# Stores of the second half's products, outputs and sums issued some steps later, pools that wait tile by tile, and four places for the front's sums

## The chip, the cores and the metric

The kernel runs on one core of one Trainium2 chip. The metric is the device time of one execution in microseconds (us); lower is better. All data starts and ends in HBM. The engines are TensorE (PE, with its weight loads as PEld), VectorE (DVE), ScalarE (ACT), GpSimd (POOL) and SyncE (SP). SP does no arithmetic here: it issues every DMA of the kernel, one after the other, from one queue.

## The reference, cut to what matters

One sequence of 1024 tokens with 1024 channels passes two layers, in fp32:

```python
for l in range(2):
    h = rms_norm(x, g0) * (1 + sc_m) + sh_m
    if l == 0: y = conformer_conv(h)             # 1024 -> 2048, GLU, causal conv of 31, layer norm, silu, 1024 -> 1024
    else:      y = diff_attention(h, k, v)       # k, v = rms_norm(x) @ w_k, @ w_v
    x = x + g_m * rms_norm(y, g1)
    h = rms_norm(x, g2) * (1 + sc_f) + sh_f
    y = conv_ffn(h)                              # u = conv3(h @ w_in): 1024 -> 2*2816;  (silu(g) * v) @ w_out
    x = x + g_f * rms_norm(y, g3)

def diff_attention(h, k, v):                     # 8 heads, two score maps each, causal
    q = h @ w_q
    s = q_c . k_c * scale + bias(distance)       # c = 0, 1
    a = softmax(s_0) - lam * softmax(s_1)
    return rms_norm(a @ v) * (1 - lambda_init) @ w_o
```

## The kernel before

**Products.** A matmul operand in fp32 is split into a rounded part and a remainder (`whi`, `wlo` of a weight, `hT` and its pair of an activation; in the second half `wh`, `wl`), and each product is three matmuls: high by high, high by low, low by high. ACT rounds (L207, L1044), POOL or DVE subtracts (L208, L1045).

**Halves.** The 1024 tokens are worked on in two halves of 512. Layer 0, the projections to Q, K and V and the first half of layer 1 are the *front part*: they are recorded in loops and put in order by the framework's scheduler, in pools opened on the stack `front` (`fc`, `wp`, `big`, `at`, `pre` and three of PSUM). `front.close()` ends them, and the *back part* begins with new pools over the same bytes: `back`, `ab`, and `psc`, `ptr`, `pav`, `pf` in PSUM. The back part holds the second half's attention, its output projection and the last FFN.

**The last FFN by sums.** The last FFN's up and down projections are formed from seven products of sums of blocks instead of eight plain ones. The sums of the weights' blocks are made on POOL and kept in HBM. `front_sums` makes those of `w_out` (11 steps of `sums_t`: two tiles of 128 x 1024 loaded, four subtractions at L940, two stores `ftd` at L942 and L943) and those of 12 of the 22 blocks of `w_in` (`sums_s`: two tiles loaded, subtractions at L951 to L957, three stores `sxd`, `syd`, `s1d` at L958 to L960), spread over the first half's attention and FFN. The other 10 are made by `First.sums` while the second half's attention runs, with the tiles `rx`, `ry` and `S`.

**The second half's attention** is written out in its order by hand (`manual_schedule`): the framework keeps each engine's instructions as the loop issues them. The loop runs over 32 steps, four for each head (one of 128 queries each), with 5 more to empty it. Step i takes the maxima of query block i (DVE), turns block i-2 (PE transposes L1203, ACT copies, DVE), exponentiates block i (ACT), issues the scores of block i+1 (PE, L1162) and, in even steps, the values of two blocks (PE, L1222 to L1224). In odd steps `First.unit` adds 12 matmuls of the last FFN (L1105 to L1107) into a bank of PSUM; every second unit, once a head, ACT copies the finished bank to a tile `X` (L1108) and it is stored as `fdx` (L1110).

In HBM, Q, K, V and the bias lie as `qd`, `kd`, `vd` and `gd`, the transposed normed rows for the last FFN as `hfd`.

**The order on SP's queue** in that loop is the order of the calls. `load_kq(h+1)` issues four loads each of Q and K (L1141, L1142) and one of the bias strip `BW` at the start of the second step of head h; `load_v(h)` issues four loads of V (L1151) at the start of its first; then come, where they fall, the store of the attention output `od` (L1227, in even steps, after ACT's copy L1226), the store `fdx`, the loads of `rx` (L1072) and `ry` (L947) and the stores of the three sums. SP is in order: a store at its head that waits for ACT or POOL holds every load behind it. Each DMA also carries one of eight numbered lanes (DMAHW0 to DMAHW7) in turn and waits until the DMA eight issues ahead of it has landed. Tiles of 4 KB a partition (Q, K, `rx`, `ry`, `X`) share 13 places, the tag `q`.

Of the kernel before, what the change touches and what calls it, by code (L numbers as in the profile page):

```python
# [12 lines left out]
F32 = mybir.dt.float32  # L13
# [6 lines left out]
P = 128  # L20
S = 1024
# [7 lines left out]
FC = F // P  # L29
# [43 lines left out]
NWS, NSS, NQ, NHS = 12, 6, 13, 40  # L73
LA = 5
LAT = 4
QS = 10


# [34 lines left out]
def trunk(ctx: ExitStack, tc: tile.TileContext, x, mw, cols, grow, w1, w2, wk, wv, wq, wo, win, wout, relb, onehot, lamr, out):  # L113
    nc = tc.nc
    V, A, G, T = nc.vector, nc.scalar, nc.gpsimd, nc.tensor
    dma = nc.sync.dma_start
    PSUM = bass.MemoryType.PSUM
# [14 lines left out]
    def nm(s):  # L132
        uid[0] += 1
        return f"{s}_{uid[0]}"
# [250 lines left out]
    def gate_row(l, v, g, r, gdr=None):  # L385

        m = sm(8)
        yield from mod_col(l, v, m)
        V.tensor_tensor(out=m, in0=m, in1=col("normg", (l * 4 + g) * 8, 8), op=ALU.mult)
        if gdr is None:  # L390
            gdr = dr.tile([1, D], F32, name=nm("gdr"))
        dma(out=gdr[0].rearrange("(k p) -> p k", p=P), in_=m)
        if r is not None:
            dma(out=r, in_=gdr.broadcast_to([P, D]))
# [215 lines left out]
    for c in range(KC):  # L610
        g = conv(cv, c, nxt.pop(0), cA, sumA, TA, py, "y")
# [64 lines left out]
    od = [[dr.tile([P, 512], F32, name=f"od{h}_{half}") for half in range(2)] for h in range(NH)]  # L676
# [248 lines left out]
    ftd = [[dr.tile([P, D], F32, name=f"ftd{j}_{i}") for i in range(2)] for j in range(FC // 2)]  # L925
    sxd, syd = [[dr.tile([P, D], F32, name=f"{n}{q}") for q in range(FC)] for n in ("sxd", "syd")]
    s1d = [dr.tile([P, 512], F32, name=f"s1d{q}") for q in range(FC)]
# [2 lines left out]

        return t.rearrange("p (k two j) -> p two k j", two=2, j=P)

    def sums_t(j, u, v):

        dma(out=u, in_=wout[1, 0, j])
        dma(out=v, in_=wout[1, 1, j])
        yield
        u0, u1, v0, v1 = u[:, 0:512], u[:, 512:1024], v[:, 0:512], v[:, 512:1024]
        for o, a, b in ((u0, v0, u0), (v0, v1, v0), (v1, v1, u0), (u1, u1, v1)):
            G.tensor_tensor(out=o, in0=a, in1=b, op=ALU.subtract)  # L940
            yield
        dma(out=ftd[j][0], in_=u)  # L942
        dma(out=ftd[j][1], in_=v)  # L943

    def sums_s(q, x, y, s):

        dma(out=y, in_=win[1, q + FC])  # L947
        yield
        (x0, x1), (y0, y1) = [[blocks(t)[:, i] for i in range(2)] for t in (x, y)]
        s_ = s.rearrange("p (k j) -> p k j", j=P)  # L950
        G.tensor_tensor(out=s_, in0=y0, in1=y1, op=ALU.add)  # L951
        yield
        G.tensor_tensor(out=y0, in0=x0, in1=y0, op=ALU.subtract)
        yield
        G.tensor_tensor(out=x0, in0=s_, in1=x0, op=ALU.subtract)
        yield
        G.tensor_tensor(out=x1, in0=x1, in1=x0, op=ALU.subtract)  # L957
        dma(out=sxd[q], in_=x)  # L958
        dma(out=syd[q], in_=y)
        dma(out=s1d[q], in_=s)  # L960
        yield

    def front_sums():
        def p4():
            return pre_.tile([P, 1024], F32, tag="p4", bufs=2, name=nm("p4"))
        for j in range(FC // 2):
            yield from sums_t(j, p4(), p4())
        for q in range(QS, FC):
            x = p4()
            dma(out=x, in_=win[1, q])  # L970
            yield from sums_s(q, x, p4(), pre_.tile([P, 512], F32, tag="p2", bufs=1, name=nm("p2")))

    pre_ = front.enter_context(tc.tile_pool(name="pre", bufs=1))
    gd_m1, gd_f1 = [dr.tile([1, D], F32, name=f"gdrow{n}") for n in range(2)]
# [4 lines left out]
    f = ffn(0, 1, hB, yB, gn_f0, ssB)  # L979
    interleave(itertools.islice(f, 60), (attn(at, 0, ssqA), NAT, 0, AE),  # L980
               (chain(gate_row(1, 2, 1, gn_m1, gd_m1), mod_scale(1, 4, 2, s_f1), mod_col(1, 3, sh_f1),
                       gate_row(1, 5, 3, None, gd_f1)), 32, 0, 60), (front_sums(), 5 * (FC // 2) + 6 * (FC - QS), 0, 60))
    ynA = wo_norm(ssqA)
    actA = []
    alongside(f, wo_pre(0, ynA, gpair, actA))
# [6 lines left out]
    front.close()  # L992


    back = ctx.enter_context(tc.tile_pool(name="back", bufs=1))
    att = ExitStack()
    ab = att.enter_context(tc.tile_pool(name="ab", bufs=1))
    psc = att.enter_context(tc.tile_pool(name="psc", bufs=2, space=PSUM))
    ptr = att.enter_context(tc.tile_pool(name="ptr", bufs=1, space=PSUM))
    pav = att.enter_context(tc.tile_pool(name="pav", bufs=1, space=PSUM))  # L1000
    pf = att.enter_context(tc.tile_pool(name="pf", bufs=1, space=PSUM))
    opool, bpool = [None], [None]

    def b2k(name="s"):
        return back.tile([P, 512], F32, tag="s", bufs=NSS, name=nm(name))

    def b4k(name="q", dt=F32):
        return back.tile([P, 1024], dt, tag="q", bufs=NQ, name=nm(name))
# [54 lines left out]
    fdx = [dr.tile([P, D], F32, name=f"fdx{q}") for q in range(FC)]  # L1063

    class First:
# [20 lines left out]
        def sums(self, q):  # L1086

            x = self.raws.pop(q)
            if q < QS:
                yield from sums_s(q, x, b4k("ry"), b2k("S"))  # L1090

        def unit(self, mk):

            q, i = divmod(self.u, 2)
            self.u += 1
            if q >= FC:
                return
            if i == 0:
                self.ps, self.x = mk(), b4k("X")
            hi, lo = self.pairs.pop((q, i))  # L1100
            ps = self.ps
            for j in range(4):
                ah, al = H[1 + i][j]
                w, v = hi[:, j * P:(j + 1) * P], lo[:, j * P:(j + 1) * P]
                T.matmul(ps, lhsT=w, rhs=ah, start=(i == 0 and j == 0), stop=False, skip_group_check=True)  # L1105
                T.matmul(ps, lhsT=w, rhs=al, start=False, stop=False, skip_group_check=True)
                T.matmul(ps, lhsT=v, rhs=ah, start=False, stop=(j == 3), skip_group_check=True)  # L1107
            A.copy(self.x[:, (1 - i) * 512:(2 - i) * 512], ps)  # L1108
            if i == 1:
                dma(out=fdx[q], in_=self.x)  # L1110

    first = First()
    bg = []

    def tick(n=1):
        for _ in range(n):
# [30 lines left out]
    def load_v(h):  # L1147
        Vh = [ab.tile([P, 8, P], F32R, tag=f"V{hl}", bufs=2, name=nm("V")) for hl in range(2)]
        for hl in range(2):
            for half in range(2):  # L1150
                dma(out=Vh[hl].bitcast(F32)[:, half * NT:(half + 1) * NT, :],  # L1151
                    in_=vd[half][:, :, hl, h * P:(h + 1) * P].rearrange("k p e -> p k e"))
        VV[h] = Vh
# [61 lines left out]
    def values(h, pr):  # L1215

        ah, al = AV[pr]
        nkb = NT + 2 * pr + 2
        po = pav.tile([P, 512], F32, tag="av", name=nm("Pav"))
        Vh = VV[h]  # L1220
        for kb in range(nkb):
            T.matmul(po[:, 0:256], lhsT=Vh[0][:, kb, :], rhs=ah[:, kb, :], start=(kb == 0), stop=False, skip_group_check=True)  # L1222
            T.matmul(po[:, 0:256], lhsT=Vh[0][:, kb, :], rhs=al[:, kb, :], start=False, stop=False, skip_group_check=True)
            T.matmul(po[:, 0:256], lhsT=Vh[1][:, kb, :], rhs=ah[:, kb, :], start=False, stop=(kb == nkb - 1), skip_group_check=True)  # L1224
        o = b2k("o")
        A.copy(o[:, 0:256], po[:, 0:256])  # L1226
        dma(out=od[h][1][:, pr * 256:(pr + 1) * 256], in_=o[:, 0:256])  # L1227
        sq = b2k("sq")
        A.activation(sq[:, 0:256], po[:, 0:256], AF.Square)
        return po, sq  # L1230
# [35 lines left out]
    for i in range(NTL + 5):  # L1266
        if i % NT == 1 and i // NT + 1 < NH:
            load_kq(i // NT + 1)
        if i % NT == 0 and i < NTL:
            load_v(i // NT)  # L1270
        if i < NTL:
            maxima(i)
        if 0 <= i - 2 < NTL:
            turned(i - 2)
        if i < NTL:
            exps(i)
        if i + 1 < NTL:
            scores(i + 1, 0)
            scores(i + 1, 1)
        t = i - 3  # L1280
        if i % 2 == 0 and 0 <= t < NTL:
            pairs[t] = values(t // NT, (t % NT) // 2)
        if t - 1 in pairs:
            squares(*pairs[t - 1])
        more(i)
        if 0 <= i - 2 < NTL:
            turned_lo(i - 2)
        if 0 <= i - 1 < NTL:
            difference(i - 1)
        if t - 1 in pairs:  # L1290
            V.tensor_copy(ss[:, t - 2:t], pairs.pop(t - 1)[0][:, 256:258])


    v = bsm(NTL)
    V.scalar_tensor_tensor(out=v, in0=r0, scalar=2.0 * HD * EPS, in1=r0, op0=ALU.mult, op1=ALU.mult)
# [1 line left out]
    yn = bnewton(v, NTL)  # L1297
    inorder.__exit__(None, None, None)
    att.close()
    opool[0] = ctx.enter_context(tc.tile_pool(name="op", bufs=1))  # L1300
    bpool[0] = ctx.enter_context(tc.tile_pool(name="bp", bufs=1, space=PSUM))


    bplan["pool"] = 0.4
# [51 lines left out]
    y, ss2 = [b4k("y") for _ in range(NT)], bsm(8)  # L1356
# [25 lines left out]
    for nh in range(2):  # L1382
        ps = [bank("Py") for _ in range(NT)]
        for pr in range(4 if nh == 0 else 2):
            w = wo_weights(nh, pr)
# [9 lines left out]
    w = [wo_weights(1, pr) for pr in (2, 3)]  # L1395
# [146 lines left out]
    y, ss2 = [], bsm(16)  # L1542
# [29 lines left out]
    n, late = FC // 2, 6  # L1572
# [127 lines left out]
```

## Time and profile before

| | |
|---|---|
| median of 3 runs | 2668.21 us (2660.86 to 2669.43) |
| the profiled execution | 2669.41 us |
| its span in the trace | 2667.6 us |
| PE busy, share of the span | 2400.3 us, 90% |
| DVE, ACT, POOL busy | 72%, 43%, 36% |
| DMA traffic | 499.54 MB, mean 187 GB/s |
| mean granted clock of TensorE | 0.963 |

The span runs from the first to the last instruction of one execution, on which all rows below are taken; the time of the execution is 1.8 us longer. "Busy" counts instructions in work; the granted clock is the share of full speed (1.00 is 2.4 GHz, 0.50 is 1.2 GHz), averaged over a stretch. Idle time in a row is put down to what ended it: `<- DMA K<-kd` is a wait that ended when a load of K landed.

### The profile page before, as it was taken

What the parts mean: (1) busy time and instruction counts of PE and PEld (TensorE: products, weight loads), DVE (VectorE), ACT (ScalarE), POOL (GpSimd) and SP (SyncE); (2) the same over time, 40 slices, a digit from 0 to 9 for tenths busy, and PEclk for the clock granted to TensorE, in tenths of its full rate; (3) what the DMA queues carried; (4) which work ended last, traced back from release to release, by engine and by line L of the source; (5) the groups of instructions that cost most, each with busy time, mean ns of one, the idle gap of its engine ahead of it and who ended that gap; (6) DMA issues with size and microseconds to landing.
All of it is one profiled execution on the core that took longest, in us unless ns stands there. A gap on an engine that the chain in (4) does not pass through costs nothing. (4 is left out here: it accounts for less than half of the span.)

```text
span 2667.6 us, 30514 instructions
## 1 busy us (share of the span) xinstructions
PE 2400.3 (90%) x10346; PEld 1887.5 (71%) x10346; DVE 1924.2 (72%) x3072; ACT 1137.7 (43%) x1871; POOL 962.3 (36%) x578
## 2 busy tenths in 40 slices
PE   5998889999988988898889999787899899999997
PEld 4666667777766766776767777576777677777875
DVE  6998689999778346757757771366664799997556
ACT  4434244332444235535534352254543544444543
POOL 2234334444534453554544323142242211213221
PEclk9999999999999998999999999898999999999999
DMA  7123643434345776677776356688863645555656
GB/s 274 56 64 111 216 163 103 156 121 128 103 140 186 268 270 201 223 252 231 237 234 231 126 184 195 193 242 239 222 230 119 234 174 186 190 197 193 198 184 218
DMA packets 204811, 499.54 MB, mean 187 GB/s; under 512 B 24432, under 2 KB 64752, under 8 KB 204656
## 3 DMA queue, kind: packets, MB, share of 16 engines
q1 hardware_dynamic: 204656, 497.60, 57.2%
q8 instruction: 82, 1.34, 0.2%
q14 instruction: 73, 0.60, 0.1%
HBM read 375.61 MB, written 121.91 MB: 187 GB/s over the span
## 5 line engine op out<-in xcount | busy, mean ns | idle before, releaser
L208 POOL TENSOR_TENSOR wlo<-raw,whi 128x1024 fp32r<-128x1024 f32 x204 | 509.3, 2498 | 758.3 <-ACT whi L207 738.1
L207 ACT CAST whi<-raw 128x1024 fp32r<-128x1024 f32 x234 | 244.9, 1047 | 466.9 <-issue 249.2
L228 PE MATMUL Pu<-hT,whi 128*128 128x512 f32 x832 | 341.6, 411 | 27.1 <-DVE tap L426 16.7
L230 PE MATMUL Pu<-hT,wlo 128*128 128x512 f32 x832 | 338.7, 407 | 12.7 <-POOL wlo L208 10.9
L229 PE MATMUL Pu<-hT,whi 128*128 128x512 f32 x832 | 337.7, 406 | 3.3 <-DVE hT L308 3.2
L493 DVE SCALAR_TENSOR_TENSOR Pcv<-cu,sv,Pcv 128x512 f32<-128x512 f32 x432 | 299.8, 747 | 3.5 <-PE Pcv L488 2.6
L243 PE MATMUL Py<-whi,gT 128*128 128x512 f32 x608 | 247.6, 408 | 15.6 <-DVE yf L447 9.5
L244 PE MATMUL Py<-wlo,gT 128*128 128x512 f32 x608 | 244.2, 402 | 7.7 <-POOL wlo L208 7.7
L245 PE MATMUL Py<-whi,gT 128*128 128x512 f32 x608 | 243.1, 400 | 0.5 <-DVE gT L185 0.5
L228 PEld LDWEIGHTS Pu<-hT,whi 128*128 128x128 f32 x832 | 161.3, 194 | 71.0 <-issue 20.4
L230 PEld LDWEIGHTS Pu<-hT,wlo 128*128 128x128 f32 x832 | 161.3, 194 | 55.2 <-POOL wlo L208 14.6
L363 DVE CUSTOM_DVE_ANT_0 mraw<-mraw,crow 128x1024 f32<-128x1024 f32 x96 | 149.1, 1554 | 68.0 <-DMA mraw<-in_mw_dram 67.9
L229 PEld LDWEIGHTS Pu<-hT,whi 128*128 128x128 f32 x832 | 161.4, 194 | 41.3 <-DVE hT L308 4.5
L243 PEld LDWEIGHTS Py<-whi,gT 128*128 128x128 f32 x608 | 116.8, 192 | 45.3 <-issue 14.5
L244 PEld LDWEIGHTS Py<-wlo,gT 128*128 128x128 f32 x608 | 116.9, 192 | 36.0 <-POOL wlo L208 9.9
L245 PEld LDWEIGHTS Py<-whi,gT 128*128 128x128 f32 x608 | 116.4, 191 | 28.3 <-DVE gT L185 1.0
L1045 DVE TENSOR_TENSOR op<-raw,op 128x512 fp32r<-128x512 f32 x115 | 91.8, 823 | 60.9 <-ACT op L1044 53.6
L1044 ACT CAST op<-raw 128x512 fp32r<-128x512 f32 x154 | 93.1, 621 | 85.4 <-DMA raw<-fad 27.9
L1589 PE MATMUL Py<-op,op 128*128 128x512 f32 x308 | 121.6, 395 | 6.7 <-ACT op L1044 5.8
L1590 PE MATMUL Py<-op,op 128*128 128x512 f32 x308 | 122.2, 397 | 4.3 <-POOL op L1045 3.5
L1591 PE MATMUL Py<-op,op 128*128 128x512 f32 x308 | 121.0, 393 | 0.0
L1045 POOL TENSOR_TENSOR wl<-rx,wh 128x512 fp32r<-128x512 f32 x44 | 58.1, 1338 | 169.8 <-ACT wh L1044 169.5
(327 smaller groups left out, 5715.3 us busy)
## 6 DMA issues: line engine op xcount, KB each, us to landing
mraw<-in_mw_dram SPq DMA_DIRECT2D x96, 512.0 KB, 5.0
raw<-in_win_dram SPq DMA_DIRECT2D x88, 512.0 KB, 4.1
raw<-in_w_dram SPq DMA_DIRECT2D x48, 512.0 KB, 3.6
raw<-in_wout_dram SPq DMA_DIRECT2D x44, 512.0 KB, 4.0
raw<-fad SPq DMA_DIRECT2D x77, 256.0 KB, 3.8
K<-kd SPq DMA_DIRECT2D x48, 256.0 KB, 7.2
V<-vd SPq DMA_DIRECT2D x48, 256.0 KB, 6.0
p<-in_win_dram SPq DMA_DIRECT2D x24, 512.0 KB, 5.4
```

The source lines that it names most:

```text
L207: A.copy(hi, raw)
L208: e.tensor_tensor(out=lo, in0=raw, in1=hi.bitcast(F32), op=ALU.subtract)
L228: T.matmul(ps, lhsT=a, rhs=ah, start=(k == 0), stop=False)
L229: T.matmul(ps, lhsT=a, rhs=al, start=False, stop=False)
L230: T.matmul(ps, lhsT=b, rhs=ah, start=False, stop=(k == KC - 1))
L243: T.matmul(ps[t], lhsT=a, rhs=rh, start=(f == 0), stop=False)
L244: T.matmul(ps[t], lhsT=a, rhs=rl, start=False, stop=False)
L245: T.matmul(ps[t], lhsT=b, rhs=rh, start=False, stop=(f == n - 1))
L363: V.tensor_tensor_reduce(out=raw, in0=raw, in1=crow, scale=1.0, scalar=0.0, op0=ALU.mult, op1=ALU.add, accum_out=r[:, k:k + 1])
L493: V.scalar_tensor_tensor(out=ps, in0=u[:, j:j + 512], scalar=col("dw", j * 8 + c), in1=ps, op0=ALU.mult, op1=ALU.add)
L1045: e.tensor_tensor(out=lo, in0=src, in1=hi.bitcast(F32), op=ALU.subtract)
L1590: T.matmul(ps[t], lhsT=a, rhs=bl, start=False, stop=False, **more_)
```

## The change

Three parts. First, the pools of the back part, and `op` and `bp` that follow it, are opened with `reuse_waits="tile"`: a tile waits for the tiles whose bytes it takes over, not for all that lay in the closed pools. Second, in the second half's attention the stores are put on a list and issued at the head of a later step, behind that step's loads: `fdx` and `od` one step later, the three sums two steps later. Third, `front_sums` has four places for its 4 KB tiles instead of two and two for its 2 KB tile instead of one, and holds the stores of one step until the next step has issued its loads.

```diff
+NPRE = 4
...
-    def sums_t(j, u, v):
+    def sums_t(j, u, v, st):
...
-        dma(out=ftd[j][0], in_=u)
-        dma(out=ftd[j][1], in_=v)
+        st(ftd[j][0], u)
+        st(ftd[j][1], v)
...
-        dma(out=sxd[q], in_=x)
-        dma(out=syd[q], in_=y)
-        dma(out=s1d[q], in_=s)
+        st(sxd[q], x)
+        st(syd[q], y)
+        st(s1d[q], s)
...
-    def front_sums():
+    def front_sums(js, qs):
+
         def p4():
-            return pre_.tile([P, 1024], F32, tag="p4", bufs=2, name=nm("p4"))
-        for j in range(FC // 2):
-            yield from sums_t(j, p4(), p4())
-        for q in range(QS, FC):
+            return pre_.tile([P, 1024], F32, tag="p4", bufs=NPRE, name=nm("p4"))
+        held = []
+
+        def st(out, in_):
+            held.append((out, in_))
+
+        def flush(n):
+            while len(held) > n:
+                o, i = held.pop(0)
+                dma(out=o, in_=i)
+        for j in js:
+            g = sums_t(j, p4(), p4(), st)
+            next(g)
+            flush(0)
+            yield
+            yield from g
+        for q in qs:
...
-    back = ctx.enter_context(tc.tile_pool(name="back", bufs=1))
+    back = ctx.enter_context(tc.tile_pool(name="back", bufs=1, reuse_waits="tile"))
...
-                yield from sums_s(q, x, b4k("ry"), b2k("S"))
+                yield from sums_s(q, x, b4k("ry"), b2k("S"), lambda o, i: store(o, i, 2))
...
-                dma(out=fdx[q], in_=self.x)
+                store(fdx[q], self.x)
...
+    def store(out, in_, steps=1):
+
+        if now[0] is None:
+            dma(out=out, in_=in_)
+        else:
+            waiting.append((now[0] + steps, out, in_))
+
+    def stores(step):
+
+        now[0] = step
+        due = [w for w in waiting if step is None or w[0] <= step]
+        waiting[:] = [w for w in waiting if step is not None and w[0] > step]
+        for _, o, i in due:
+            dma(out=o, in_=i)
...
-        dma(out=od[h][1][:, pr * 256:(pr + 1) * 256], in_=o[:, 0:256])
+        store(od[h][1][:, pr * 256:(pr + 1) * 256], o[:, 0:256])
...
         if i % NT == 0 and i < NTL:
             load_v(i // NT)
+        stores(i)
         if i < NTL:
             maxima(i)
```

**One head on SP's queue.** The next two pieces are SyncE's rows from one head's last `od` store to the middle of the next head's Q and K loads, in the steady part of the attention loop. The line numbers of the changed kernel are 1 to 40 higher; every deferred store has the line of its one issuing statement, L1150. What stands in brackets is what the row waits for: a DMA lane, or another engine. Before:

```order
L1227 DMA od_1_5570<-o_14061 128x256 [waits DMAHW2_49,Activation_49]
L1110 DMA fdx_13091<-X_13988 128x1024 [waits DMAHW3_49,Activation_49]
L1072 DMA rx_14112<-in_win_dram 128x1024 [waits DMAHW4_49]
L947 DMA ry_14122<-in_win_dram 128x1024 [waits DMAHW5_49,PE_49]
L1151 DMA V_14131<-vd_5563 128x4x128 [waits DMAHW6_49,PE_49]
L1151 DMA V_14131<-vd_5564 128x4x128 [waits DMAHW7_49]
L1151 DMA V_14132<-vd_5563 128x4x128 [waits DMAHW0_49,PE_49]
L1151 DMA V_14132<-vd_5564 128x4x128 [waits DMAHW1_49]
L1227 DMA od_1_5572<-o_14183 128x256 [waits DMAHW2_49,Activation_49]
L1141 DMA Q_14196<-qd_1_5550 64x1024 [waits DMAHW3_49]
L1142 DMA K_14194<-kd_5560 64x1024 [waits DMAHW4_49]
```

The same place in the changed kernel:

```order
L1150 DMA od_1_5570<-o_14058 128x256 [waits DMAHW2_49,Activation_49]
L1092 DMA rx_14111<-in_win_dram 128x1024 [waits DMAHW3_49]
L948 DMA ry_14121<-in_win_dram 128x1024 [waits DMAHW4_49,PE_49]
L1188 DMA V_14130<-vd_5563 128x4x128 [waits DMAHW5_49,PE_49]
L1188 DMA V_14130<-vd_5564 128x4x128 [waits DMAHW6_49]
L1188 DMA V_14131<-vd_5563 128x4x128 [waits DMAHW7_49,PE_49]
L1188 DMA V_14131<-vd_5564 128x4x128 [waits DMAHW0_49]
L1150 DMA fdx_13091<-X_13988 128x1024 [waits DMAHW1_49,Activation_49]
L1178 DMA Q_14195<-qd_1_5550 64x1024 [waits DMAHW2_49]
L1179 DMA K_14193<-kd_5560 64x1024 [waits DMAHW3_49]
```

The `fdx` store has moved behind `rx`, `ry` and the four loads of V; the `od` store that stood ahead of the Q and K loads has moved behind all eight of them and the load of `BW`.

**The seam between the parts.** These are SyncE's rows around the back part's first loads, before:

```order
L305 DMA hfd_12124<-hf_13038 128x512 [waits DMAHW7_49,Activation_49]
L713 DMA vd_5564<-hl_13053 256x1x512 [waits DMAHW0_49,DVE_49]
L713 DMA vd_5564<-hl_13057 256x1x512 [waits DMAHW1_49,DVE_49]
L1141 DMA Q_13129<-qd_1_5540 64x1024 [waits DMAHW3_49,DMAHW2_49,DMAHW4_49,DMAHW1_49,DMAHW5_49,DMAHW0_49,DMAHW6_49,DVE_49,DMAHW7_49,PE_49,Pool_49]
L1142 DMA K_13127<-kd_5555 64x1024
```

and in the changed kernel:

```order
L306 DMA hfd_12124<-hf_13038 128x512 [waits DMAHW7_49,Activation_49]
L714 DMA vd_5564<-hl_13053 256x1x512 [waits DMAHW0_49,DVE_49]
L714 DMA vd_5564<-hl_13057 256x1x512 [waits DMAHW1_49,DVE_49]
L1178 DMA Q_13129<-qd_1_5540 64x1024 [waits DMAHW2_49]
L1179 DMA K_13127<-kd_5555 64x1024 [waits DMAHW4_49,DMAHW3_49,DMAHW7_49,DVE_49,PE_49]
L1178 DMA Q_13129<-qd_1_5540 64x1024
L1179 DMA K_13127<-kd_5555 64x1024 [waits DMAHW5_49]
L1178 DMA Q_13130<-qd_1_5540 64x1024 [waits DMAHW6_49,PE_49]
L1179 DMA K_13128<-kd_5555 64x1024
L1178 DMA Q_13130<-qd_1_5540 64x1024 [waits DMAHW0_49]
L1179 DMA K_13128<-kd_5555 64x1024 [waits DMAHW1_49]
```

The one wait for everything has become a wait of each load for what lay in its bytes; the lanes of the last two stores of `vd` (0 and 1) are now waited for by the seventh and eighth load.

**The front's sums on POOL.** GpSimd's rows where the first sums stand, before (the second step's sums follow twelve rows of `wlo` further on):

```order
L940 TENSOR_TENSOR p_1260_7227<-p_1261_7228,p_1260_7227 128x512
L940 TENSOR_TENSOR p_1261_7228<-p_1261_7228 128x512
L940 TENSOR_TENSOR p_1261_7228<-p_1261_7228,p_1260_7227 128x512
L940 TENSOR_TENSOR p_1260_7227<-p_1260_7227,p_1261_7228 128x512
L333 COPY xt_6039<-ym_5589 1x1
L208 TENSOR_TENSOR wlo_6219<-raw_6216,whi_6218 128x1024
```

and in the changed kernel:

```order
L941 TENSOR_TENSOR p_1260_7227<-p_1260_7227,p_1261_7228 128x512
L941 TENSOR_TENSOR p_1297_7377<-p_1298_7378,p_1297_7377 128x512
L334 COPY xt_6039<-ym_5589 1x1
L941 TENSOR_TENSOR p_1298_7378<-p_1298_7378 128x512
L941 TENSOR_TENSOR p_1298_7378<-p_1298_7378,p_1297_7377 128x512
L209 TENSOR_TENSOR wlo_6219<-raw_6216,whi_6218 128x1024
L334 COPY xt_6046<-ym_5590 1x1
L941 TENSOR_TENSOR p_1297_7377<-p_1297_7377,p_1298_7378 128x512
```

The second step's sums now stand directly behind the first's, ahead of and around the subtraction of the weight `wlo_6219`; the later steps stand some rows earlier, too. The number of instructions on PE, DVE, ACT and POOL and the number of DMAs are unchanged.

## Rows read from the trace of the kernel before

**Rows 1.** Windows: busy time of five engines, granted clock, DMA share, GB/s.

```profile
1721.90:1749.00 27.10, 22.88 (x97) 18.29 (x98) 15.78 (x30) 14.52 (x26) 10.80 (x8) 0.85 1.05 278
1749.00:1947.00 198.00, 161.59 (x916) 138.25 (x915) 129.01 (x237) 101.49 (x195) 62.78 (x46) 0.91 0.81 229
```

**Rows 2.** Waits of TensorE, 1749 to 1947 us: total, times, longest.

```profile
PE Psc L1162 <- DMA K<-kd: 16.8, 5, 4.2
PE Ptr L1203 <- DVE p L1193: 10.0, 8, 2.2
PE Psc L1162 <- DVE p L1193: 5.5, 2, 2.8
```

**Rows 3.** Timeline of TensorE around one wait: start, duration, instruction, idle before.

```profile
1892.07 0.94 PE L1162 MATMUL Psc<-K,Q 128*128 128x512 f32 x4 [2.71 <-DVE p L1193]
...
1893.53 0.39 PE L1106 MATMUL Pf<-hT,wh 128*128 128x512 f32 x1
1893.76 0.42 PE L1107 MATMUL Pf<-hT,wl 128*128 128x512 f32 x1
...
1895.68 0.63 PE L1106 MATMUL Pf<-hT,wh 128*128 128x512 f32 x1
1896.11 0.63 PE L1107 MATMUL Pf<-hT,wl 128*128 128x512 f32 x1
```

**Rows 4.** Timeline of SyncE's queue and of ScalarE ahead of it.

```profile
1871.09 0.32 SPq L1110 DMA_DIRECT2D fdx<-X  x1
...
1875.96 2.41 SPq L1227 DMA_DIRECT2D od<-o  x1
1878.42 0.45 SPq L1141 DMA_DIRECT2D Q<-qd  x1
...
1883.66 0.59 SPq L1142 DMA_DIRECT2D K<-kd  x1
...
1870.48 0.59 ACT L1108 COPY X<-Pf 128x512 f32<-128x512 f32 x1 [6.12 <-PE Pf L1107]
```

**Rows 5.** Waits of SyncE's queue, 1749 to 1947 us.

```profile
SPq L1110 <- ACT X L1108: 57.4, 7, 12.0
```

**Rows 6.** DMA view, 1707 to 1976 us: traffic in 40 slices; issue to landing.

```profile
GB/s 351 161 239 342 205 284 347 248 307 212 99 155 269 293 215 222 157 315 223 264 168 309 225 256 144 315 226 274 135 292 206 291 90 304 129 140 256 38 308 174
...
K<-kd SPq DMA_DIRECT2D x32, 256.0 KB, 7.9
...
fdx<-X SPq DMA_DIRECT2D x11, 512.0 KB, 3.0
...
vd<-hl SPq DMA_DIRECT2D x3, 512.0 KB, 4.1
```

**Rows 7.** Timeline of SyncE's queue and of TensorE at the seam.

```profile
1708.32 0.33 SPq L305 DMA_DIRECT2D hfd<-hf  x1
1708.74 1.68 SPq L713 DMA_DIRECT2D vd<-hl  x2
1714.38 0.50 SPq L1141 DMA_DIRECT2D Q<-qd  x1
...
1721.94 1.62 PE L1162 MATMUL Psc<-K,Q 128*128 128x512 f32 x4 [14.51 <-DMA K<-kd]
1726.56 2.05 PE L1162 MATMUL Psc<-K,Q 128*128 128x512 f32 x5 [3.00 <-DMA K<-kd]
```

**Rows 8.** Front's sums, 780 to 1540 us: waits of TensorE, GpSimd, SyncE's queue.

```profile
PE Pu L230 <- POOL wlo L208: 9.1, 6, 3.7
...
PE Py L244 <- POOL wlo L208: 6.0, 3, 5.1
...
POOL p L940 <- DMA p<-in_wout_dram: 53.9, 8, 14.0
...
SPq L942 <- POOL p L940: 41.6, 6, 9.8
```

**Rows 9.** Timeline of GpSimd: half of one step's subtractions.

```profile
839.22 2.67 POOL L940 TENSOR_TENSOR p<-p,p 128x512 f32<-128x512 f32 x2
```

More of the change, by code (lines that the diff above doesn't have):

```diff
@@ L941, in sums_t, with sums_s @@
             yield
-        dma(out=ftd[j][0], in_=u)
-        dma(out=ftd[j][1], in_=v)
-    def sums_s(q, x, y, s):
+        st(ftd[j][0], u)
+        st(ftd[j][1], v)
+    def sums_s(q, x, y, s, st):
         dma(out=y, in_=win[1, q + FC])
@@ L957, in sums_s @@
         G.tensor_tensor(out=x1, in0=x1, in1=x0, op=ALU.subtract)
-        dma(out=sxd[q], in_=x)
-        dma(out=syd[q], in_=y)
-        dma(out=s1d[q], in_=s)
+        st(sxd[q], x)
+        st(syd[q], y)
+        st(s1d[q], s)
         yield
-    def front_sums():
+    def front_sums(js, qs):
         def p4():
-            return pre_.tile([P, 1024], F32, tag="p4", bufs=2, name=nm("p4"))
-        for j in range(FC // 2):
-            yield from sums_t(j, p4(), p4())
-        for q in range(QS, FC):
+            return pre_.tile([P, 1024], F32, tag="p4", bufs=NPRE, name=nm("p4"))
[13 more added lines that the diff above has]
+        for q in qs:
             x = p4()
             dma(out=x, in_=win[1, q])
-            yield from sums_s(q, x, p4(), pre_.tile([P, 512], F32, tag="p2", bufs=1, name=nm("p2")))
+            g = sums_s(q, x, p4(), pre_.tile([P, 512], F32, tag="p2", bufs=NPRE // 2, name=nm("p2")), st)
+            next(g)
+            flush(0)
+            yield
+            yield from g
+        flush(0)
     pre_ = front.enter_context(tc.tile_pool(name="pre", bufs=1))
@@ L981, in trunk @@
                (chain(gate_row(1, 2, 1, gn_m1, gd_m1), mod_scale(1, 4, 2, s_f1), mod_col(1, 3, sh_f1),
-                       gate_row(1, 5, 3, None, gd_f1)), 32, 0, 60), (front_sums(), 5 * (FC // 2) + 6 * (FC - QS), 0, 60))
+                       gate_row(1, 5, 3, None, gd_f1)), 32, 0, 60), (front_sums(range(FC // 2), range(QS, FC)), 5 * (FC // 2) + 6 * (FC - QS), 0, 60))
     ynA = wo_norm(ssqA)
@@ L992, in trunk @@
     front.close()
-    back = ctx.enter_context(tc.tile_pool(name="back", bufs=1))
+    back = ctx.enter_context(tc.tile_pool(name="back", bufs=1, reuse_waits="tile"))
     att = ExitStack()
[L997 to L1001, printed above, removed]
+    ab = att.enter_context(tc.tile_pool(name="ab", bufs=1, reuse_waits="tile"))
+    psc = att.enter_context(tc.tile_pool(name="psc", bufs=2, space=PSUM, reuse_waits="tile"))
+    ptr = att.enter_context(tc.tile_pool(name="ptr", bufs=1, space=PSUM, reuse_waits="tile"))
+    pav = att.enter_context(tc.tile_pool(name="pav", bufs=1, space=PSUM, reuse_waits="tile"))
+    pf = att.enter_context(tc.tile_pool(name="pf", bufs=1, space=PSUM, reuse_waits="tile"))
     opool, bpool = [None], [None]
@@ L1109, in unit @@
             if i == 1:
-                dma(out=fdx[q], in_=self.x)
+                store(fdx[q], self.x)
     first = First()
     bg = []
+    waiting = []
+    now = [None]
+    def store(out, in_, steps=1):
[9 more added lines that the diff above has]
+            dma(out=o, in_=i)
     def tick(n=1):
@@ L1291, in trunk @@
             V.tensor_copy(ss[:, t - 2:t], pairs.pop(t - 1)[0][:, 256:258])
+    stores(None)
     v = bsm(NTL)
@@ L1299, in trunk @@
     att.close()
-    opool[0] = ctx.enter_context(tc.tile_pool(name="op", bufs=1))
-    bpool[0] = ctx.enter_context(tc.tile_pool(name="bp", bufs=1, space=PSUM))
+    opool[0] = ctx.enter_context(tc.tile_pool(name="op", bufs=1, reuse_waits="tile"))
+    bpool[0] = ctx.enter_context(tc.tile_pool(name="bp", bufs=1, space=PSUM, reuse_waits="tile"))
     bplan["pool"] = 0.4
```

## The prediction

> **What bounds the kernel now.** The profile page comes first: TensorE is busy for 2400.3 of 2667.6 us, so no edit off TensorE gains anything unless TensorE waits for it, and the whole room is 267 us of idle time and whatever runs at the lower clock. The next thing to read is who TensorE waits for in the three places that the change touches.
>
> The largest is the second half's attention. From 1749 to 1947 us, 198 us that hold seven changes of head, TensorE is busy for 161.6 us [rows 1]. The waits name the rest: 16.8 us in five waits of the scores for loads of K, 5.5 us in two waits of the scores put down to DVE's L1193, and 10.0 us of the transposes for the same L1193 [rows 2]. The second of these is to be read with care. One of its two stands at 1892.07 [rows 3], ahead of the second group of a new head's first scores. These need no result of L1193 but the second K tile, whose last load was issued at 1883.66 [rows 4]; with the 7.9 us that a load of K takes to land [rows 6] that is 1891.6. So it is a wait for K, too, and the loads of K cost 16.8 + 5.5 = 22.3 us in seven waits.
>
> Why K is late is seen on SyncE's queue [rows 4]: the store `fdx` goes out at 1871.09, when ACT's copy of `X` has ended (1870.48 + 0.59). Behind it stand `rx`, `ry`, four loads of V and the store `od`, which is held until 1875.96 and takes 2.41 us; the first load of Q follows at 1878.42, the last of K 5.2 us after it. The queue's waits agree: 57.4 us, in seven waits, at `fdx` for ACT [rows 5]. In this time the loads behind it do nothing.
>
> The wait has a tail. The matmuls of L1106 and L1107 start 0.23 us apart just after it (1893.53, 1893.76), and 0.43 us apart a little later (1895.68, 1896.11) [rows 3]: TensorE's granted clock falls from its upper level, 2.4 GHz, to its lower, 1.2 GHz, after a wait of 2.71 us. Some nine matmuls of the twelve run so, 9 x 0.2 = 1.8 us a head. The mean granted clock of the seven stretches is 0.91 [rows 1]. The Trainium skill (TensorE: Matmul & The Clock Gate, "Part 1: The HAM clock gate") says that the engine's clock is halved when it has been idle and comes back only with work, so that a wait costs more than its length; by that rule the seven waits are worth their tails too, and by bare waits alone they would not be. The trace agrees with the rule (0.43 against 0.23 us), and the two sums are 35 and 22 us.
>
> **The change part by part.**
>
> *Stores in the attention loop.* Nothing is removed; the stores of `fdx`, `od` and the sums move behind loads on one queue. What each now precedes: `rx`, `ry` and V no longer wait for `X`. They go out in the stretch up to 1871 in which the queue stood still. `fdx` itself still stands ahead of Q and K, and still waits for ACT. So Q and K start where `fdx` now starts plus its 0.4 us: 1871.5 in place of 1878.42, 7 us earlier. The last K goes out 5.2 us on, at 1876.7, and lands at 1884.6; TensorE asks for it at 1892.07 - 2.71 = 1889.4 [rows 3, 4, 6]. That leaves 4.8 us to spare. One load in each group takes over the bytes of `X` or its lane and waits until `fdx` has landed, 3.0 us [rows 6], which is less than the 3 us or so that the four or five loads ahead of it need to be issued: nothing. The `od` store held back by one step lies beside the next step's work; only the last heads' `od` is read soon after, and there TensorE works on the last products. At most 1 us, inside the range. The waits of K go, 22.3 us, and with them the tail, 7 x 1.8 = 12.6 us: 35 us at most, a loop of 163 us.
>
> What may give some of it back is the traffic. The 198 us move 229 GB/s x 198 = 45.3 MB [rows 1]. The highest rate that a whole head has shown is 278 GB/s, in the first one, with a DMA share of 1.05; at that rate the bytes need 163 us, the same as TensorE. Slices of 7 us go up to 351 GB/s [rows 6], so 278 is not a wall, but two bounds that meet are seldom both reached, and landings grow when the queues are full. The Trainium skill (DMA: Bandwidth & Descriptors, "Specifications") puts HBM's limit for one core at about 358 GB/s; by that, an estimate of 127 us, traffic would not bind and the loop would gain its 35 us. No run here shows that rate over a head. At the other end, if half of the waits come back as other waits (the transposes' 10.0 us on L1193 show where: with a shorter period DVE's chain has less time) and no tail is saved, 11 us. I take the middle, rather below: **21 us** of 11 to 35.
>
> *Pools that wait by tile.* At the seam TensorE has nothing to do for 14.51 us before the first scores and 3.00 us before the second [rows 7]. The first load of Q goes out at 1714.38 because it waits for all of the front's pools, the last stores of `vd` among them, which were issued by 1710.42 and take 4.1 us to land [rows 6, 7]. Now it waits for tiles long free, and can go at 1710.5. The first K waits for the store `hfd` of 1708.32 (landing near 1711.4 by 3.0 us), the seventh and eighth load for the lanes of the last two `vd`, near 1714; before, those two were six and seven places behind 1714.38, at the 5.2 / 7 = 0.75 us a place of [rows 4] from 1718.9. So the scores move by 3.9 to 4.9 us: **4 us**. The lower bound is 3, if the stores of `vd` share the DMA engines with the loads; more than 5 there cannot be. The pools `op` and `bp` after the loop: nothing to 1 us.
>
> *The front's sums.* GpSimd waited 53.9 us for tiles of `w_out` that came late, with weights' `wlo` behind them in its order, and SyncE's queue stood 41.6 us at L942 for the sums, with weights' loads behind [rows 8]. Four places and later stores undo both. But what TensorE sees of it is 9.1 + 6.0 = 15.1 us of waits for `wlo` [rows 8], and not all of those have a sum ahead of them. Upper bound 15. Lower bound: one step's sums take 2 x 2.67 = 5.3 us on GpSimd [rows 9], and now two steps stand in a row at the start; if a `wlo` that TensorE awaits is behind them once, -5. I take a third of the upper bound: **5 us**.
>
> The sum is made against the profiled execution, 2669.4 us (span 2667.6 and 1.8 around it), 1.2 us above the median: 2669.4 - 21 - 4 - 5 = **2639 us**. The ends give 2669.4 - 11 - 3 + 5 = 2660 and 2669.4 - 35 - 5 - 15 = 2614. About 0.3%, 8 us, is what a measurement of this kernel can tell from no change.
>
> **The rivals.**
>
> *Traffic keeps the period.* The loop's waits for K become waits for later landings, or for DVE's L1193, and the clock tail stays because some wait of 2 us remains. For it: DMA share 0.81 over stretches in which TensorE stood 18% [rows 1]. Against it: 4.8 us of slack, and slices well over 300 GB/s [rows 6]. The loop gains 6 to 11, the seam 3, the front 0: about 2657 (2655 to 2660).
>
> *TensorE's floor is reached.* The loop at 163 us, the front gains 10: 2669.4 - 35 - 4 - 10 = 2620 (2614 to 2628). For it: nothing but K makes long waits in the loop [rows 2]. Against it: both bounds of 163 us would have to hold together. The two rules of the skill, of the clock and of HBM's limit, lead here.
>
> *The stall only moves.* Q and K still stand behind `fdx`, and `fdx` behind ACT's copy. If `rx`, `ry` or V are not free to go before 1871 (V's places come free with the values of two heads before, `ry`'s with scores), the block moves as a whole and Q starts near 1878 as before: only the seam's 4 us, 2665. V is four loads and 3 us, so this needs a place that comes free over 5 us later than I read it.
>
> *Slower.* In the front, 23 steps of sums are now made one step earlier on GpSimd, each 5.3 us [rows 9]. If, at each, a `wlo` that TensorE needs comes behind the sums rather than ahead, TensorE waits up to 5.3 us in each. To end 8 us above the time before, that must eat the 25 us of loop and seam and 8 more: 33 / 23 = 1.4 us a step. With 2 us in each, 2669 - 25 + 46 = 2690. For it: six waits of `Pu` and three of `Py` on `wlo` exist already, up to 5.1 us [rows 8]. Against it: `wlo` mostly waits for ACT, so GpSimd has room.
>
> **How the numbers follow.** The forecast, 2629 to 2652, has 0.60; traffic 0.16; TensorE's floor 0.12; the stall that moves 0.06; slower 0.06. The range leaves out the last two and the edges of the second and third: 2620 to 2661. Faster by over 0.3%: forecast, floor, and most of the traffic case, 0.85; same: the rest of it and the moved stall, 0.09; slower 0.06.
>
> **What would show it.** In the profile after: Q's first load of a steady head less than 1 us behind `fdx`; the scores' waits for K in the loop under 5 us; L1106 and its neighbours 0.23 us apart through the head, the mean clock of the loop at 0.95 or more; a head in some 25 us in place of 198 / 7 = 28; the first load of Q some 4 us closer to the last `vd`; GpSimd's waits for `w_out` below 20 us. I am wrong in the loop if the scores wait for K as before or if a new wait of over 2 us a head stands on L1193; wrong in the front if waits for `wlo` rise above 15 us.

## The result, and the profile after

The changed kernel takes 2620.6 us (median of 4 runs, 2619.1 to 2623.6), the kernel before 2664.6 us beside it: a ratio of 0.9835, 95% interval 0.9813 to 0.9858. Measured again beside the last experiments, it was 2621.1 us and 0.9815 (0.9793 to 0.9838). That is 44 us faster, at the lower edge of the range and 18 us below the forecast of 2639.

Where the time went is best read by following the same matmul through both traces. TensorE has 10346 in each run; the table gives the start of the n-th, counted from the first. In the front the order of a few differs, so a single row there is good to some us.

| matmul | stage | before, us | after, us | difference |
|---|---|---|---|---|
| 3000 | front, sums begin | 824.6 | 825.3 | +0.8 |
| 4000 | first half's attention and FFN | 1095.4 | 1096.6 | +1.1 |
| 5000 | the same | 1346.1 | 1332.4 | -13.7 |
| 5400 | just behind the front's sums | 1452.5 | 1423.1 | -29.4 |
| 6470 | first scores of the back part | 1721.9 | 1688.8 | -33.2 |
| 6567 | first head done | 1749.1 | 1716.3 | -32.8 |
| 7481 | last heads | 1947.2 | 1894.5 | -52.7 |
| 8200 | last FFN | 2137.5 | 2093.3 | -44.2 |
| 10345 | end | 2655.8 | 2610.0 | -45.8 |

So the front gave 31 us (its last store of `vd` had been issued by 1710.42, [rows 7], and is issued by 1679.46 now), the seam 2, the loop 20, and 7 were lost again behind the loop.

These are rows of one execution each, and the stages repeat to some us only. Where the loop was left as it was, the stretch from matmul 6567 to 7481 took 193.2 to 195.1 us in three further traces (e1, e3, e4 below) against 198.1 here, so 15 to 20 us of the loop are the change's. The front as changed ends 27.2 to 37.4 us early in the traces of e1, e5, e6, e8 and e11.

The next piece is the view by windows of the changed kernel, over the first head and over the stretch of the same matmuls as the second of [rows 1]; columns as there.

```profile
1688.80:1716.30 27.50, 23.03 (x98) 18.37 (x99) 15.91 (x30) 14.52 (x26) 10.82 (x8) 0.84 1.06 285
1716.30:1894.50 178.20, 155.33 (x915) 137.95 (x914) 135.96 (x235) 101.23 (x195) 64.45 (x46) 0.93 0.87 254
```

The 198.0 us have become 178.2; TensorE's own busy time fell by 6 us and its idle time by 14, the share of DMA rose from 0.81 to 0.87. The clock stayed low, 0.93 after 0.91. TensorE's waits in that stretch tell why; they answer to [rows 2]:

```profile
PE Ptr L1240 <- DVE p L1230: 22.1, 7, 3.3
PE Psc L1199 <- DVE sm L1210: 0.4, 2, 0.2
PE Ptr L1240 <- DVE ss L1329: 0.3, 1, 0.3
```

All waits for K are gone, 22.3 us of them; the transposes' waits for DVE's L1230 (L1193 before) have grown from 10.0 to 22.1 us, one of 3.3 us in each head. SyncE's queue in a steady head (answering to [rows 4]):

```profile
1815.13 0.32 SPq L1150 DMA_DIRECT2D od<-o  x1
1815.49 0.43 SPq L1092 DMA_DIRECT2D rx<-in_win_dram  x1
1816.02 0.40 SPq L948 DMA_DIRECT2D ry<-in_win_dram  x1
1816.52 2.05 SPq L1188 DMA_DIRECT2D V<-vd  x4
1820.66 0.33 SPq L1150 DMA_DIRECT2D fdx<-X  x1
1821.04 0.45 SPq L1178 DMA_DIRECT2D Q<-qd  x1
...
1825.84 0.60 SPq L1179 DMA_DIRECT2D K<-kd  x1
```

The first load of Q follows `fdx` by 0.4 us, as forecast, and `ry` now goes out right behind `rx`, well ahead of `fdx`. That early `ry` has a price. These are VectorE and GpSimd in the same head:

```profile
1817.54 1.15 DVE L1230 SCALAR_TENSOR_TENSOR p<-p,sm,p 128x896 f32<-128x896 f32 x1
...
1823.70 1.32 DVE L1228 SCALAR_TENSOR_TENSOR sm<-r,neglam,sm 128x1 f32<-128x1 f32 x1
1825.06 2.37 DVE L1230 SCALAR_TENSOR_TENSOR p<-p,sm,p 128x1024 f32<-128x1024 f32 x1
1827.36 0.94 DVE L1210 CUSTOM_DVE_ANT_0 p<-Psc,BW 128x768 f32<-128x768 f32 x1
```

```profile
1821.23 2.55 POOL L1065 TENSOR_TENSOR wl<-rx,wh 128x512 fp32r<-128x512 f32 x2 [18.18 <-ACT wh L1064]
1823.74 1.27 POOL L952 TENSOR_TENSOR S<-ry 128x512 f32<-128x512 f32 x1
1825.09 1.26 POOL L954 TENSOR_TENSOR ry<-rx,ry 128x512 f32<-128x512 f32 x1
1826.43 2.14 POOL L956 TENSOR_TENSOR rx<-S,rx 128x512 f32<-128x512 f32 x1
```

L1228 works on one element a partition and took 0.22 us wherever GpSimd stood still; beside GpSimd's first sum it takes 1.32, until that sum ends at 1825.01. L1230, 1024 wide, takes 2.37 us: it runs on for 1.1 us after the second sum has ended, and the third sum, which begins beside it, takes 2.14 us where its neighbours take 1.27. These rows look like turns, one whole instruction waiting for the other. L1210, which reads PSUM and SBUF, is not stretched (0.94 us for 768 here, 0.95 before). In the kernel before, GpSimd's sums of a head came later, mostly beside the narrowest difference:

```profile
1847.19 1.28 DVE L1193 SCALAR_TENSOR_TENSOR p<-p,sm,p 128x1024 f32<-128x1024 f32 x1
...
1852.36 2.00 DVE L1193 SCALAR_TENSOR_TENSOR p<-p,sm,p 128x640 f32<-128x640 f32 x1
```

Over the seven heads, a sum ran beside the 1024 wide difference once before and in every head after the change. With `ry` in time, GpSimd goes straight from the weights' remainder to the sums, and these fall on the widest difference of the head, for which TensorE waits 2.6 to 3.3 us. The Trainium skill (GPSIMD Engine Reference, "1. Specifications") says that GpSimd's access to SBUF is shared with VectorE and that an instruction of VectorE with two inputs in SBUF contends for it; the trace agrees on both sides (L1228 and L1230 have two such inputs, L1210 has one).

### The profile page after: what moved, and what is told of

The parts are those of the page before. It is cut to its first block, busy times and chain, and to the rows that moved or that the text cites. A ratio compares the mean times of both kernels' runs of the same rounds, so it can differ in the third digit from the quotient of the medians.

```text
span 2621.8 us, 30492 instructions
## 1 busy us (share of the span) xinstructions
PE 2390.0 (91%) x10346; PEld 1885.3 (72%) x10346; DVE 1925.6 (73%) x3072; ACT 1138.3 (43%) x1871; POOL 952.4 (36%) x578
```

## The experiments

Each was timed against the kernel before on the same chip; times are medians.

**The three parts alone.** e1 has the front's sums as in the change, and neither the pools nor the deferred stores:

```diff
-    back = ctx.enter_context(tc.tile_pool(name="back", bufs=1, reuse_waits="tile"))
+    back = ctx.enter_context(tc.tile_pool(name="back", bufs=1))
...
-        if now[0] is None:
-            dma(out=out, in_=in_)
-        else:
-            waiting.append((now[0] + steps, out, in_))
+        dma(out=out, in_=in_)
```

> The front's sums alone as in the change (four places, stores held for a step); pools and the attention loop as before. Theory: the front alone makes the first 31 of the 45 us, by loads that are no longer queued behind stores that wait for GpSimd; 2664.6 - 31 = 2634 us, and the first load of Q of the back part stands 31 us earlier. Rival (the 5 us of the prediction stand, and the tile-wise pools let the front end earlier): 2658 to 2662.

2629.9 us against 2665.6, ratio 0.9856 (0.9829 to 0.9883): 36 us. In its trace matmul 6440, near the end of the front, starts 32.6 us earlier than before (31.0 in the changed kernel). The front alone makes most of the change.

e2 has the deferred stores alone (`NPRE = 2`, the front's stores issued at once, no `reuse_waits`):

> The deferred stores in the second half's attention alone. Theory: 20 us in the loop, of which some 6 are lost again behind it, 2664.6 - 14 = 2651 (2645 to 2655), with the wait of the transposes for DVE's L1230 up from 10 to over 20 us. Rival (the loop gains only when it starts early, from the seam): within 4 us of before.

2654.1 us, ratio 0.9947 (0.9929 to 0.9965): 14 us by the ratio, 11 by the medians. By the matmuls' starts it gains 18.8 us from 6600 to 7400 and gives back 4.5 of them by 7640, as the changed kernel does (4.7); it also needs no early start. The first theory stands.

e3 has the tile-wise pools alone:

> The pools that wait tile by tile alone. Theory: the first scores come 2 to 4 us earlier and the loop, which waits for K as before, keeps it: 2661 to 2663, hardly told from no change. Rival (it also frees the front's scheduler): over 10 us faster.

2661.8 us, ratio 0.9990 (0.9973 to 1.0006): not told from no change. In its trace matmul 6520 is 2.9 us early where 6440 was 0.7 early, so the seam gives some 2 us. By the medians the three parts alone come to 36 + 11 + 4 = 51 us and the whole change to 44; as each is known to 4 to 7 us only, the two aren't told apart.

**What in the front does it.** e4 has four places (and two), the stores issued at once, nothing else:

```diff
-            held.append((out, in_))
+            dma(out=out, in_=in_)
```

> Four places (and two) for the front's sums, their stores issued at once as before; nothing else. Theory A (the places do it: loads for the next step need not wait for the last step's stores): near e1, 2634. Theory B (the holding does it: SyncE's queue stands at a store that waits for GpSimd): near before, 2660, with the queue's waits for GpSimd at the stores still some 90 us in 780 to 1540.

2653.6 us, ratio 0.9954 (0.9936 to 0.9973): 12 us, between the two theories. Places and holding both count. Its queue still stands at these stores; SyncE's waits in e4, 780 to 1540 us:

```profile
SPq L971 <- POOL p L958: 40.8, 7, 8.6
...
SPq L971 <- POOL p L941: 24.6, 6, 6.5
...
SPq L971 <- POOL p L954: 8.6, 3, 3.1
```

That is 74.0 us, where the kernel before had 41.6 at L942 [rows 8] and 34.2, 10.5 and 10.5 at L958, L959 and L943 (96.8 in all), and e1 7.8 at one of the held stores. Standing times of 97, 74 and 8 us go with gains of 0, 12 and 36; with the waits at the same stores that bear a load's or another name they are 107, 92 and 8. A part of the standing only moved: at the loads of weights, which wait until GpSimd's `wlo` has read the tile that they overwrite, the queue stood 137.4 us before, 188.7 in e4 and 197.9 in e1.

e7 takes the stores from SyncE's queue in another way: two places as before, stores issued on GpSimd's queue:

```diff
-            held.append((out, in_))
+            nc.gpsimd.dma_start(out=out, in_=in_)
```

> The kernel before, with the front's stores of sums issued on GpSimd's own queue right behind the sums, two places and the rest as before. SyncE's queue then holds no store that waits for GpSimd. If the queue's standing at these stores is what cost the front (theory B), most of e1's 36 us: 2632 to 2645. If it is the two places (theory A), the loads still wait for the stores' landing: 2650 to 2662. GpSimd's own cost of issuing 58 DMAs, not seen in any row yet, comes off either.

2686.8 us, ratio 1.0075 (1.0054 to 1.0095): slower, which neither theory had. SyncE's queue now stands at the next loads instead, since with two places they wait for the stores to land:

```profile
SPq L985 <- DMA syd<-p: 44.5, 6, 8.1
...
SPq L936 <- DMA ftd<-p: 16.5, 4, 6.5
```

61.0 us at the head of the queue, and 16.8 more in two shorter rows. The standing was moved, not removed, so this run doesn't separate the two; what GpSimd pays for issuing was not measured apart. Held stores with two places were not run.

e10 keeps the change and leaves the front's sums out:

> The changed kernel with the front's block sums left out (23 steps of four GpSimd operations; the loaded tiles are stored as they are, s1d gets half of a tile), loads and stores kept. What GpSimd's sums still cost the front behind the change: if TensorE waits for wlo behind them or VectorE is slowed by them, 10 to 25 us less than the changed kernel, 2596 to 2611; if the front is now held by loads and by its own chains, within 4 us of it, 2617 to 2625.

2583.7 us, ratio 0.9683 (0.9662 to 0.9703): 37 us less than the changed kernel, more than I had allowed for. From matmul 3800 to 5400, where the changed kernel needs 380.6 us:

```profile
1027.30:1386.40 359.10, 341.11 (x1602) 276.40 (x1602) 245.52 (x650) 196.05 (x334) 93.00 (x64) 0.99 0.83 256
```

The loads were all kept and DMA's share rose to 0.83 (0.76 in the changed kernel), so traffic is not what holds the front: GpSimd's sums still are, by their time on the engine or by the order that the scheduler finds around them. Part of it is the shared access; VectorE's L431, one element a partition, with two inputs in SBUF, takes 559 ns in the changed kernel and 213 without the sums:

```profile
L431 DVE SCALAR_TENSOR_TENSOR tap<-fhist,sv,tap 128x1 f32<-128x1 f32 x36 | 20.1, 559 | 0.2
```

```profile
L431 DVE SCALAR_TENSOR_TENSOR tap<-fhist,sv,tap 128x1 f32<-128x1 f32 x40 | 8.5, 213 | 0.3
```

TensorE's waits say in part how much of the 37 us is that and how much is `wlo` standing behind sums on GpSimd: from 780 to 1540 us those for VectorE's L827, a difference with two inputs in SBUF, fall from 17.3 to 5.4 us, those for `wlo` from 11.7 to 6.0. The rest of the 37 us isn't split.

**What holds the loop now.** e6 is the changed kernel without the loop's sums; loads and stores are kept:

> The changed kernel with the loop's block sums left out (four GpSimd operations a head; the loaded tiles are stored as they are, and s1d gets half of ry), all loads and stores kept. Theory of the shared access: L1228 and L1230 keep 0.22 and 1.2 us, the transposes' waits for L1230 fall from 27 to under 6 us, the loop gains 10 to 16 us: 2605 to 2611. Rival (VectorE's chain, or traffic): waits and loop as in the changed kernel, 2618 to 2623.

2590.2 us, ratio 0.9710 (0.9686 to 0.9733): 30 us less than the changed kernel, of which 6 lie in the front, where nothing was changed. From matmul 6567 to 7481 it needs 154.8 us (198.1 before, 178.2 with the change). VectorE's one-element instruction is back at a mean of 231 ns (511 in the changed kernel), the 1024 wide difference at 1284 (2353), the transposes' waits for it in this stretch at 7.5 us (22.1), and the clock at 1.00 (0.93):

```profile
1709.20:1864.00 154.80, 145.49 (x916) 128.40 (x915) 118.70 (x235) 101.54 (x195) 17.85 (x14) 1.00 0.98 294
```

The loop runs at 294 GB/s over this stretch: traffic at the changed kernel's 254 is no bound.

e5 keeps all the work and only starts the loop's sums a step later, so that the load of `ry` stands behind `fdx`:

```diff
             if q < QS:
+                for _ in range(3):
+                    yield
                 yield from sums_s(q, x, b4k("ry"), b2k("S"), lambda o, i: store(o, i, 2))
...
-        tick(2)
+        tick(3)
```

> The changed kernel, with the loop's sums begun one step later: the load of ry stands behind fdx instead of beside rx, so GpSimd's four operations of a head run later. Theory (GpSimd's sums slow two of VectorE's instructions with both tensors in SBUF, L1228 from 0.22 to 1.32 us and the 1024 wide L1230 from 1.2 to 2.37, and this makes TensorE's new wait of 3.3 us a head): the long durations move to other, narrower instructions, the waits of the transposes for L1230 fall from 27 to under 12 us, and the loop gains 8 to 14 us on the changed kernel: 2607 to 2613. Rival (VectorE's chain is too long for the shorter period anyway): the waits stay, 2618 to 2623.

2609.4 us, ratio 0.9781 (0.9761 to 0.9801): 11 us less than the changed kernel, as the theory had it. Its VectorE rows in one head:

```profile
1824.38 1.28 DVE L1232 SCALAR_TENSOR_TENSOR p<-p,sm,p 128x1024 f32<-128x1024 f32 x1
1829.29 1.16 DVE L1230 SCALAR_TENSOR_TENSOR sm<-r,neglam,sm 128x1 f32<-128x1 f32 x1
1830.48 2.01 DVE L1232 SCALAR_TENSOR_TENSOR p<-p,sm,p 128x640 f32<-128x640 f32 x1
```

```profile
1829.13 1.30 POOL L952 TENSOR_TENSOR S<-ry 128x512 f32<-128x512 f32 x1 [4.94 <-DMA Q<-qd]
1830.51 1.30 POOL L954 TENSOR_TENSOR ry<-rx,ry 128x512 f32<-128x512 f32 x1
1831.88 1.74 POOL L956 TENSOR_TENSOR rx<-S,rx 128x512 f32<-128x512 f32 x1
```

In this head the stretching has moved to the 640 wide difference, the narrowest, behind which TensorE waits at most 0.8 us. It is so in four of the seven heads; in two the 1024 wide one is still stretched (2.27 and 2.37 us), and in others the sums fall on 768 and 896. The stretch of matmuls 6567 to 7481 falls from 178.2 to 167.9 us, its clock rises to 0.98, and the transposes' waits from 1675 to 1900 us fall from 22.9 to 15.5 us (I had said from 27 to under 12).

e8 is the changed kernel with only `od` deferred in the loop:

```diff
-                store(fdx[q], self.x)
+                dma(out=fdx[q], in_=self.x)
```

> The changed kernel with only od deferred in the loop; fdx and the sums' stores go out at once as before. Theory: od is what held Q and K furthest; V's loads follow fdx at 1871 and Q and K come 3 us earlier than before, landing 1 to 2 us before TensorE asks at the old period and just late at the shorter one: half of the loop's gain, 2626 to 2632. Rival (fdx holds them just as much): K's waits stay above 15 us, 2632 to 2637.

2630.4 us, ratio 0.9861 (0.9838 to 0.9885): 10 us behind the changed kernel, a time that the theory allowed. But TensorE's waits for K in 1675 to 1900 us are 29.5 us in seven, of which 12.3 is the seam's: 17.2 us in the loop, and its gain from 6600 to 7400 is 2.8 us of 19.8, no more than e1 shows there with the loop unchanged (3.7). So moving `od` alone is not enough, as long as `fdx` with what stands behind it holds Q and K; the waits are the rival's. The rows before had shown it: of the 7.3 us from `fdx` to the first load of Q only 2.4 are `od`'s [rows 4]. Moving `fdx` alone was not run.

**Moving sums between front and loop.** e9 has the sums of 16 blocks in the front and 6 in the loop, on e5 (`QS = 6`):

> The kernel of e5, with the sums of 16 blocks of w_in made in the front and of 6 in the attention loop (12 and 10 before). If sums cost the loop what e6 shows (30 us for 10, 3 us each) and the front less, since GpSimd has idle time there: 2597 to 2607. If the front pays as much for them (its stage is bound by the same loads and engines): 2607 to 2615.

2648.3 us, ratio 0.9916 (0.9894 to 0.9939): 39 us slower than e5, worse than both expectations. The front ends 44.7 us later than e5's (matmul 6440), and TensorE's waits for the transposes' DVE chain and for `wlo` are up (27.8, 10.1 and 6.6 us in 780 to 1540, after 20.3, 6.7 and 5.9 in e5); they explain a part of it only. The loop, with four sums fewer, gains 1.7 us.

e12 goes the other way, `QS = 14`:

> The kernel of e5 with the sums of 8 blocks of w_in in the front and of 14 in and behind the attention loop (12 and 10 before). By e9, four more steps in the front cost 39 us, and by e10 the 23 steps there still cost 37; four fewer should give back 10 to 30, and the loop pays 0 to 3 us for one more sum (the loop has 11 blocks, the last 3 fall behind it, where DMA and GpSimd have room): 2585 to 2603. If e9's loss came from the order that the scheduler found and not from the number of sums: within 5 us of e5's 2609.

2625.2 us, ratio 0.9843 (0.9821 to 0.9866): 16 us slower than e5 and outside both expectations. The front ends within 2 us of e5's, so fewer steps there give nothing back that the spread of some us would let see; between matmuls 7400 and 7720, where three sums now fall behind the loop, it needs 10 us more. The front's cost is not a price a step. The order that the scheduler makes around the sums may matter as much as their number; no run shows it. The changed kernel again, beside these two on a chip:

> The changed kernel itself, beside the other two on one chip: 2617 to 2624, so that e5 (2609) is told from it.

It gave 2621.1 us, as said above. Its interval and that of e5, 0.9793 to 0.9838 and 0.9761 to 0.9801, overlap by 0.0008; that of the first measurement, 0.9813 to 0.9858, lies clear of e5's.

## Why the prediction was right, and where its sum was not

The median lies inside the range by 0.6 us, and that it does is partly luck: the front gained 31 us, outside its stated bounds of -5 to 15, while the loop came out at its forecast and 7 us were lost behind it. The rival that named 2620 us, TensorE's floor, gave the same time by another way: a loop of 163 us and 10 us from the front, where 178.2 and 31 were measured.

*The seam: 4 us forecast, 2 measured.* The first load of Q goes out at 1679.51, directly behind the last `vd` as worked out. But the queue then needs 6.4 us for the eight loads where it took 5 (the second, K, alone 1.15 us), with the stores of `vd` still landing (the last at 1683.60), and the first load lands in 5.4 us where it took 3.5. The scores' two waits answer to [rows 7]:

```profile
1688.76 1.62 PE L1199 MATMUL Psc<-K,Q 128*128 128x512 f32 x4 [12.30 <-DMA K<-kd]
1693.67 3.76 PE L1199 MATMUL Psc<-K,Q 128*128 128x512 f32 x10 [3.29 <-issue]
```

14.51 has become 12.30; the second is 3.29 after 3.00. The step that said that both scores move with the loads' issue failed by half, and the lower bound of 3, meant for this sharing, was too high.

*The loop: 21 us forecast, 20 measured (177 and 178.2 us for the stretch).* Size and first half of the mechanism were right: Q 0.4 us behind `fdx`, no wait for K left. Half of what that gave, 12 us, returned as waits for L1193's successor, 3.3 us a head. That was in the sum, but a new wait of over 2 us a head there was also the prediction's own sign of being wrong in the loop. The reason I gave for these was only that VectorE has less time in a shorter period. The runs show another: GpSimd's sums, moved by the earlier `ry`, stretch the widest L1230 (e5, e6). The mean clock of 0.95 or more did not come, 0.93, since a wait of 3.3 us a head remains. Nor did traffic bind: the "bound" of 163 us at 278 GB/s was passed by e6, 154.8 us at 294 GB/s.

*Behind the loop: nothing to 1 us forecast, 7 lost.* From matmul 7880 to 8200, 3 us are lost in e1 and e3 as well (3.7 and 3.9), which change nothing there, but 0.0 in e4 and 1.1 in the changed kernel's second trace (e11): this place differs from execution to execution. Another 4.7 us, from 7400 to 7640, are the change's: e2 has it (4.5), e5 and e6 hardly (1.7 and 1.4 at most). It begins with a wait of the transposes for L1230 of 4.53 us in the last head, 2.42 before; in e5, with the sums moved, it is 2.40 again, so this too is the sums'.

*The front: 5 us forecast, 31 measured, 36 alone (e1).* This is the term that was mis-sized. I bounded it by TensorE's waits put down to `wlo`, 15.1 us [rows 8], and took a third. The waits put down to other names went as well. This is the stretch of matmuls 3800 to 5400, before and after:

```profile
1039.00:1452.50 413.50, 358.70 (x1601) 287.24 (x1600) 282.62 (x637) 196.94 (x336) 200.67 (x132) 0.93 0.72 235
1042.50:1423.10 380.60, 349.49 (x1602) 281.34 (x1600) 272.75 (x640) 197.85 (x337) 182.78 (x127) 0.97 0.76 246
```

TensorE's idle time fell from 54.8 to 31.1 us, and of this 23.7 only 3 to 4 are `wlo`'s (9.2 before, 5.7 after); most of the rest stood at VectorE's rows (`tap` 8.1 us, `ssqA` 9.1 to 3.9, and others). Its busy time fell by another 9.2, at a clock of 0.97 after 0.93. A late load can reach TensorE through any in-order engine. The largest single wait before shows it: VectorE stands for a `mraw`, the `tap` comes behind it, and TensorE's wait bears the name of `tap`.

```profile
1048.48 2.71 DVE L363 CUSTOM_DVE_ANT_0 mraw<-mraw,crow 128x1024 f32<-128x1024 f32 x1 [8.52 <-DMA mraw<-in_mw_dram]
1052.01 0.77 PE L228 MATMUL Pu<-hT,whi 128*128 128x512 f32 x1 [8.10 <-DVE tap L426]
```

The right bound was all idle time of the stage and its clock. e1 and e4 show that the change in the front causes the gain. Which link carries the rest is not shown. That `mraw` had been issued at 1035.03 and took 13.4 us to land, and from 1022 us on the queue had stood at no store of the sums; weights were not late at ScalarE, which waits for no load in this stretch before and for 4.0 us after. The edit also changed the order that the scheduler gave to GpSimd's rows, and no run holds that order fixed.

The slower rival, sums ahead of a `wlo` that TensorE needs, did not come true: its waits fell. That the sums still cost the front 37 us (e10) was in no step. GpSimd's waits for tiles of `w_out`, which were to fall from 53.9 to under 20 us, fell to 37.4. The forecast's 2639 was made against one execution, and by the profiled one after, 2623.6, it was 16 us off: the front (+26), less the seam (-2), the loop (-1) and the part behind it (-7). The median is 3 us lower still.

## What to carry to other kernels

On a queue that issues in order, ask of each store what it waits for and which loads stand behind it; moving it behind loads that are already free adds no work and brings them forward. When a stage is full of in-order engines, the waits that bear the loaded tile's name are no upper bound of what a change in the loads can give (15 us here, where 31 came): the bound is all idle time of the stage and its clock. A load that comes earlier also starts the engine that waits for it earlier: look at what runs beside it then; here, moving that start by one step was worth another 11 us.

## What the runs showed of the hardware

GpSimd and VectorE slow each other by whole instructions, however little there is to do: an instruction of VectorE on a single element a partition took 1.32 us beside a GpSimd sum, until that sum ended, and 0.22 without. Its two inputs lie in SBUF; an instruction of VectorE with one input in PSUM kept its 0.94 us beside GpSimd. And the loop moved 294 GB/s for 155 us without its sums (e6) and, in single slices of 6 us of the changed kernel's attention, up to 391.

```profile
GB/s 291 258 231 341 237 253 359 379 222 264 355 311 217 391 365 296 240 187 285 295 217 223 211 314 218 276 202 318 220 279 189 268 117 95 174 200 172 60 265 135
```
